# One branch over two rare paths, tiles normalised into PSUM, and constant products ahead of mixer two

## The chip, the cores and the metric

The kernel runs on one core of one Trainium2 chip. Its time is device microseconds from start to end of one execution; several executions were timed, and one more was taken with the hardware profiler. The engines are TensorE (PE, and PEld for its weight loads), VectorE (DVE), ScalarE (ACT), GpSimd (POOL) and SyncE (SP, which here issues most DMAs). A "q" behind a name (ACTq) is that engine's sequencer: branches, register loads, semaphore events.

## The reference

A trunk of two layers on 512 tokens of 1024 values, all in float32. Each layer is a mixer and a mixture of experts, each followed by a layer norm of the scaled input plus the result:

```python
for layer in range(2):
    mix = mixer[layer](x)                  # layer 0: convolutions; layer 1: gated blocks and chunked attention
    x = layer_norm(ALPHA * x + mix, mix_ln_g[layer], mix_ln_b[layer])
    ffn = hierarchical_moe(x, ...)         # 4 groups x 8 experts, one group, the best 2 experts of it
    x = layer_norm(ALPHA * x + ffn, ffn_ln_g[layer], ffn_ln_b[layer])

hb = silu(xb @ w_gate[e]) * (xb @ w_up[e]) # one expert: 1024 -> 512
y  = hb @ w_down[e]                        # 512 -> 1024; summed with the routing weights
layer_norm(x, g, b) = (x - mean) * rsqrt(var + 1e-5) * g + b
```

Which expert gets how many tokens depends on the data.

## The kernel before, in words

All 512 tokens stay in SBUF as four tiles of 128 tokens (`acc`, tiles t = 0 to 3). The 32 experts of a layer are taken as 16 pairs, g = 0 to 15, and every expert has 64 places for tokens. A pair is: gate products `pg` (`proj2`, L748, its products at L746), up products `pu`, the hidden values (`hidden`, L759), their transposes and eviction to `hT` by ScalarE (`hidden_T`, L764 to L769), and down products `py` (`down`, L772 to L780). In between TensorE spreads the previous pair's results back to the tokens (`combine` and `spread`, L788 to L799), and VectorE adds them to `acc`. The expert weights stream in from HBM on SP's queue, several pairs ahead.

An expert with more than 64 tokens needs extra work, and the routing counts how much, on the chip. Two pieces of code are there for it, and both are behind a branch on such a count. `overflow` (the branch at L1156, `skip`) handles a little more for one pair; the branch stands in every pair from g = 2 on, between the hidden transposes and the down products. `crowded` (from L1035, the branch at L1037) is a general loop over all pairs for what exceeds even that; it stands once per layer, before the gate products of g = 15. In the data timed here neither is needed in the last pair of a layer: the branches jump over the code. The counts lie in a row `nxi` in SBUF; each engine loads its count into a register, and the value `most`, the largest count for the general loop, is loaded at the end of g = 14 (L1164), along with a hint to TensorE's instruction fetch (`mark_branch_hint_location`). For the pairs the hint stands ahead of `pu` (L1135).

After the branch at L1037 `last()` follows: in layer 0 it issues the loads of two weight arrays of mixer two (`last0`, L1606) on SP's queue; in layer 1, constants of the last norm. `Last` (L801 to L830) finishes the sums of the last pair, with tiles 0 and 1 accumulated in PSUM by way of an identity product, and the statistics of the norm. `hat` (L281) writes the normalised values of a tile by ScalarE. Then come mixer two (L1328), whose `turn` (L1335) transposes the normalised tiles as input to its products, or, after layer 1, `output` (L1583): scale and shift by `gf` and `bf` on GpSimd and VectorE and the stores. GpSimd does tile 0 and three quarters of tile 1 (`PQ` is 256), VectorE the last quarter and tiles 2 and 3, on ScalarE's and SP's store queues.

`keep_warm` (L145) multiplies a constant with itself into a PSUM tile that nobody reads.

The order of each engine's instructions is the order in which the code is written. An instruction waits on semaphores for its inputs and for the release of the buffers it writes; behind a branch, a waiter waits for the event with which an engine closes it.

Of the kernel before, what the change touches and what calls it, by code (L numbers as in the profile page):

```python
# [10 lines left out]
I32 = mybir.dt.int32  # L11
# [17 lines left out]
NTHR = 6  # L29
WIDE = 3  # L30
CM = 1
PQ = 256
W0 = 10
W3 = 0
W4 = 0
# [8 lines left out]
def trunk(ctx: ExitStack, tc: tile.TileContext, a, out, layers=2, moe=True):  # L44
# [18 lines left out]
    def ptile(tag, shape=(128, 512)):  # L63
        return mtile(shape) if tag == "m" else ps.tile(list(shape), F32, name="p" + tag, tag=tag)

    def small(shape, name, dt=F32, **kw):
        return wk.tile([128] + list(shape), dt, name=name, **kw)
# [77 lines left out]
    def keep_warm(n, tag="m"):  # L145
        p = ptile(tag)
        for _ in range(n):
            PE.matmul(p, onesb[:, 0:1].to_broadcast([128, 128]), onesb[:, 0:1].to_broadcast([128, 512]), start=True, stop=True)
# [293 lines left out]
    class Router:  # L442
# [178 lines left out]
        def counts(self):  # L621
            c = self.rk[:, NT]
            big = wk.tile([128, NE, NE], F32, name="big", tag="xb")
            TT(big, self.at, bc(c[:, None, :], [NE, NE]), op=OP.mult)
            cs = small([NP, 2], "cs", tag="rcb")
            DVE.tensor_reduce(cs.rearrange("p g two -> p (g two)"), big, axis=AX.X, op=OP.add)
            over = small([2, NP, 2], "over", tag="scr")
            for i in range(2):
                TT(over[:, i], cs, lim[:, i], op=OP.is_gt)
            nxs = small([2 * NP + 1], "nxs")  # L630
            n, m = nxs[:, 0:NP], nxs[:, NP:2 * NP]
            mxc = small([NP], "mxc", tag="mxc")
            DVE.tensor_reduce(mxc, over[:, 1], axis=AX.X, op=OP.max)
            DVE.scalar_tensor_tensor(n, over[:, 0, :, 1], 2.0, over[:, 0, :, 0], op0=OP.mult, op1=OP.add)
            DVE.scalar_tensor_tensor(n, mxc, float(WIDE), n, op0=OP.mult, op1=OP.max)
            TS(n[:, HEAVY:HEAVY + 1], over[:, 0, HEAVY:HEAVY + 1, 1], float(WIDE), None, op0=OP.mult)
            mxe = small([NP], "mxe", tag="mxc")
            DVE.tensor_reduce(mxe, c.rearrange("p (g two) -> p g two", two=2), axis=AX.X, op=OP.max)
            nx = small([NP, NTHR], "nx", tag="scr")
            TT(nx, bc(mxe[:, :, None], [NP, NTHR]), bc(thr[:, None, :], [NP, NTHR]), op=OP.is_gt)  # L640
            DVE.tensor_reduce(m, nx, axis=AX.X, op=OP.add)
            for g in FIRST:
                DVE.scalar_tensor_tensor(m[:, g:g + 1], mxe[:, g:g + 1], float(CAP), m[:, g:g + 1], op0=OP.is_gt, op1=OP.add)
            DVE.tensor_reduce(nxs[:, 2 * NP:], m, axis=AX.X, op=OP.max)
            nxi = small([2 * NP + 1], "nxi", I32)
            DVE.tensor_copy(nxi, nxs)
            return nxi

# [99 lines left out]
    def proj2(tag, xt, wa, wb, own=EVEN[0]):  # L748
        p = ptile(tag)
        for k in range(KD):  # L750
            by_slots(p, xt[:, k], (wa[:, k], wb[:, k]), own, start=(k == 0), stop=(k == KD - 1))
        return p
# [6 lines left out]
    def hidden(sg, pu):  # L759
        h = wk.tile([128, 512], F32, name="h", tag="q1")  # L760
        DVE.tensor_mul(h, sg, pu)  # L761
        return h

    def hidden_T(h):  # L764
        p = mtile((128, 4, 128))
        for j in range(4):
            PE.transpose(p[:, j], h[:, j * 128:(j + 1) * 128], ident)  # L767
        hT = wk.tile([128, 4, 128], F32, name="hT", tag="q2")
        ACT.activation(hT, p, AF.Copy)  # L769
        return hT  # L770

# [11 lines left out]
    def onehot_S(tk, tag="q3"):  # L783
        S = wk.tile([128, T], F32R, name="S", tag=tag)
        TS(S, io, tk, None, op0=OP.is_equal)
        return S
# [6 lines left out]
    def combine(S, yh, yl, ts=range(NT)):  # L793
        for t in ts:
            for h in range(2):
                s = slice(h * 512, (h + 1) * 512)
                p = mtile()
                spread(p, S, yh, yl, t, h)
                DVE.tensor_add(acc[:, t, s], acc[:, t, s], p)  # L799
# [31 lines left out]
    def combine_last(last, mid=None):  # L831
        return last.ys, last.mrs + last.finish(2, mid)
# [135 lines left out]
    ET = mybir.EngineType  # L968

    def count(nxi, i, **kw):  # L970
        return nc.values_load(nxi[0:1, i:i + 1], min_val=0, max_val=NTHR + 1,
                              skip_runtime_bounds_check_because="a count of blocks", **kw)

    def when(nxi, i, above, engines=None):
        v = count(nxi, i, **({} if engines is None else {"engines": engines}))
        return v, tc.If(v > above)

    def experts(rt, ws, T1, pt, x1d, xt, xg, xg2, update, last, last2, lead, finish):
# [55 lines left out]

        def crowded():  # L1035
            slots = ws.order[6:8]
            with tc.If(most > 0, label=f"most{ws.l}", preferred_fallthrough_block=True):  # L1037
                for g in range(NP):
                    v, cond = when(nxi, NP + g, 0)
                    with cond:  # L1040
                        cur = small([2, NT], "cur")
                        R3, yh, yl = (wk.tile([128, D], F32R, name="room", tag=t) for t in ("l1", "xt1", "lng"))
                        R3 = R3.rearrange("p (j t m) -> p j t m", j=2, t=NT)
                        TS(cur, rt.r, 0.0 if g in FIRST else -float(CAP), None, op0=OP.add)
                        with tc.For_i(0, v, 1):
                            TS(cur, cur, -float(CAP), None, op0=OP.add)
                            rt.onehot(R3, range(NT), cur)
                            T3 = Table(rt, R3)
                            T3.one(2 * g)
                            gather(xg, x1d, T3.idx[:, 0:1])  # L1050
                            xo = gather_T(xg, rt.gb, wk.tile([128, KD, 128], F32, name="xo", tag="xb"))
                            u = [ws.fetch(0, j, slots[j], g) for j in range(2)]
                            h3 = gated(proj2("g", xo, *u))
                            u = [ws.fetch(0, 2 + j, slots[j], g) for j in range(2)]
                            h3 = hidden_T(hidden(h3, proj2("u", xo, *u)))
                            u = [ws.fetch(0, 4 + j, slots[j], g) for j in range(2)]
                            y3 = down(h3, *u, T3.wt[:, 0:1], (yh, yl))
                            combine(onehot_S(T3.tk[:, 0:1], "q2"), *y3)

        for g in range(NP):  # L1060
            W = lambda j: ws.u[6 * g + j]
            own, own2 = EVEN if COLS[g] < HEAVY else ODD
            if g == NP - 1:
                crowded()
                last()
            skip = f"skip{ws.l}_{g}"
            sg = gated(proj2("g", xt, W(0), W(1), own))
            if g == 0:
# [62 lines left out]
                h2 = wk.tile([128, 128], F32, name="h2", tag="r")  # L1131
                ACT.activation(h2, proj1("g", xo, W(0), b), AF.Silu)
            if g > 1:
                v = count(nxi, COLS[g])
                tc.mark_branch_hint_location(skip, v > 0, engines=[ET.PE])  # L1135
            pu = proj2("u", xt, W(2), W(3), own)
            h = hidden(sg, pu)
# [16 lines left out]
                down1(hT2, W(4), tw[:, 1:2], tw[:, 0:1])  # L1154
            if g > 1:
                with tc.If(v > 0, label=skip, preferred_fallthrough_block=True):  # L1156
                    overflow(v)
            ws.load(6 * g + 4 + 9)
            if g == NP - 1:
                last2()  # L1160
            if 0 < g < NP - 1:
                gather2(g + 1)
            if g == NP - 2:
                most = count(nxi, 2 * NP)  # L1164
                tc.mark_branch_hint_location(f"most{ws.l}", most > 0, engines=[ET.PE])
            if g == NP - 1:
                S = onehot_S(col(T1.tk, g))
            if g < NP - 1:
# [159 lines left out]
    def mixer1(prev, ws):  # L1328
# [29 lines left out]
                    ACT.activation(hi, x2[:, e], AF.Copy)  # L1358
                (DVE, POOL)[j % 2].tensor_tensor(lo, x2[:, e], hi, op=OP.subtract)

        ys, mrs = combine_last(prev, lambda: turn(0))
        TS(bq, par1[:, 4:8], 0.125, None, op0=OP.mult)
        gf, bf = (wk.tile([128, D], F32, name="gf", tag=t) for t in ("lng", "lnb"))
        rows = []
# [218 lines left out]
    def output(prev):  # L1583
        gf, bf = st["gf"], st["bf"]
        ys, mrs = combine_last(prev)

        def put(q, t, s):
            q.dma_start(out[t * 128:(t + 1) * 128, s], acc[:, t, s])

        def scale_shift(e, t, s):  # L1590
            x = acc[:, t, s]
            e.tensor_tensor(x, x, gf[:, s], op=OP.mult)  # L1592
            e.tensor_tensor(x, x, bf[:, s], op=OP.add)  # L1593
            put(nc.scalar, t, s)
        for t, s in ((0, slice(0, 512)), (0, slice(512, 1024)), (1, slice(0, 512)), (1, slice(512, 512 + PQ))):
            scale_shift(POOL, t, s)
        scale_shift(DVE, 1, slice(512 + PQ, 1024))
        for t in (2, 3):
            for h in range(2):
                s = slice(512 * h, 512 * h + 512)  # L1600
                x = acc[:, t, s]
                DVE.scalar_tensor_tensor(x, ys[t][h], mrs[t][0], gf[:, s], op0=OP.subtract, op1=OP.mult)  # L1602
                DVE.scalar_tensor_tensor(x, x, mrs[t][1], bf[:, s], op0=OP.mult, op1=OP.add)  # L1603
                put(nc.sync, t, s)

    def last0():  # L1606
# [103 lines left out]
```

## Time and profile before

| | us |
|---|---|
| three runs | 1438.19, 1443.88, 1445.37; median 1443.88 |
| the profiled execution | 1442.83, of which the profiled span 1440.9 |
| TensorE busy | 1333.4 (93% of the span) |
| VectorE, ScalarE, GpSimd busy | 684.5, 370.3, 294.7 |
| mean granted TensorE clock | 0.976 of full speed |
| read from HBM | 461.56 MB, 325 GB/s over the span |

A busy share is a mean over stages: in the expert stretches (about 220 to 690 us and 940 to 1420 us) TensorE and the weight stream both run almost without a break, in the mixers the other engines matter more. An "issue" as the cause of idle time means that the profile shows nothing that the engine waited for.

### The profile page before, as it was taken

The page shows a single profiled execution, that of the slowest core. Times are in us where ns is not written, and L with a number is a line of the kernel's source. Part 1 is how long each engine was busy: PE and PEld are TensorE (multiplying, and loading weights), DVE is VectorE, ACT ScalarE, POOL GpSimd, SP SyncE. Part 2 cuts the span into 40 slices and gives each one's busy share as a digit, 9 for nine tenths or more (in the row PEclk, how much of TensorE's full clock was granted, in tenths as well). Part 3 has the DMA queues.
Part 4 walks back from the last instruction along what each step waited for, and adds up shares of the span by engine and source line. Part 5 has one row for each costly group of instructions (what it writes and reads, how often), then busy time and mean ns, then how long its engine had stood idle before and what let it go on. Part 6 is the DMA issues. An engine that isn't in the chain of part 4 may idle for free. (4 is left out here: it accounts for less than half of the span.)

```text
span 1440.9 us, 19633 instructions
## 1 busy us (share of the span) xinstructions
PE 1333.4 (93%) x7322; PEld 705.9 (49%) x7322; DVE 684.5 (48%) x1412; ACT 370.3 (26%) x701; POOL 294.7 (20%) x262
## 2 busy tenths in 40 slices
PE   9989999998999998898899999999999999989984
PEld 6777764333353334333586767834333444333331
DVE  7997688323342223322628554794322343322326
ACT  5545541111111111111525555511111111111101
POOL 5784620000000000000653239200000000000002
PEclk9999999999999999999999999999999999999997
DMA  7505469999999999999500037689999999999971
GB/s 294 234 5 212 175 243 428 419 424 422 419 403 412 422 419 426 422 418 354 206 1 1 23 133 315 257 338 421 420 425 424 421 394 420 427 422 422 423 301 59
DMA packets 56837, 461.21 MB, mean 320 GB/s; under 512 B 8804, under 2 KB 9444, under 8 KB 33232
## 3 DMA queue, kind: packets, MB, share of 16 engines
q1 hardware_dynamic: 51184, 449.96, 75.8%
q0 software_dynamic: 4608, 7.79, 1.5%
q8 instruction: 102, 1.67, 0.5%
q10 hardware_dynamic: 864, 1.13, 0.2%
q14 instruction: 79, 0.65, 0.1%
HBM read 461.56 MB, written 6.29 MB: 325 GB/s over the span
## 5 line engine op out<-in xcount | busy, mean ns | idle before, releaser
L746 PE MATMUL py<-w,hT 128*64 128x512 f32 (+1 forms) x1280 | 243.2, 617 | 22.3 <-issue 11.6
L746 PE MATMUL pu<-w,xt 128*64 128x512 f32 (+1 forms) x1280 | 244.2, 607 | 19.8 <-DMA w<-in_w_up_dram 19.8
L746 PE MATMUL pg<-w,xt 128*64 128x512 f32 (+1 forms) x1280 | 233.4, 599 | 10.9 <-ACTq L1037 10.9
L761 DVE TENSOR_TENSOR h<-sg,pu 128x512 f32<-128x512 f32 x32 | 22.0, 688 | 355.9 <-issue 302.1
L691 POOL DMA_INDIRECT xg<-x1d,idx x30 | 29.7, 990 | 780.2 <-PE m L439 677.9
L746 PEld LDWEIGHTS pu<-w,xt 128*64 128x64 f32 (+1 forms) x1280 | 78.3, 129 | 176.3 <-issue 143.2
L799 DVE TENSOR_TENSOR acc<-acc,m 128x512 f32<-128x512 f32 x240 | 148.6, 680 | 19.3 <-PE m L791 17.3
L746 PEld LDWEIGHTS pg<-w,xt 128*64 128x64 f32 (+1 forms) x1280 | 76.2, 128 | 163.1 <-issue 140.8
L746 PEld LDWEIGHTS py<-w,hT 128*64 128x64 f32 (+1 forms) x1280 | 72.4, 128 | 154.5 <-issue 150.4
L780 DVE SCALAR_TENSOR_TENSOR y<-py,wt,y 128x512 fp32r<-128x512 f32 x64 | 48.0, 750 | 199.2 <-ACT y L779 199.2
L779 ACT ACTIVATE y<-py,wt 128x512 fp32r<-128x512 f32 x64 | 44.0, 687 | 302.9 <-PE py L746 302.9
L790 PE MATMUL m<-y,S 128*128 128x512 f32 x248 | 106.1, 428 | 0.0
L791 PE MATMUL m<-y,S 128*128 128x512 f32 x248 | 98.0, 395 | 0.0
L109 POOL TENSOR_TENSOR wl<-win,wh 128x512 fp32r<-128x512 f32 x64 | 84.2, 1331 | 65.6 <-ACT wh L108 65.4
L769 ACT ACTIVATE hT<-m 128x512 f32<-128x512 f32 x32 | 19.1, 597 | 292.4 <-PE m L767 270.5
L109 POOL TENSOR_TENSOR wl<-wo,wh 128x512 fp32r<-128x512 f32 x64 | 82.1, 1309 | 38.2 <-ACT wh L108 37.8
L756 ACT ACTIVATE sg<-pg 128x512 f32<-128x512 f32 x32 | 19.1, 597 | 217.3 <-PE pg L746 217.3
L790 PEld LDWEIGHTS m<-y,S 128*128 128x128 f32 x248 | 46.8, 189 | 39.3 <-issue 26.9
L128 PE MATMUL m<-xh,wl 128*128 128x512 f32 x144 | 57.6, 400 | 3.0 <-POOL wl L109 3.0
L127 PE MATMUL m<-xh,wh 128*128 128x512 f32 x144 | 57.4, 399 | 0.8 <-ACT wh L108 0.8
L129 PE MATMUL m<-xl,wh 128*128 128x512 f32 x144 | 56.8, 394 | 0.0
L791 PEld LDWEIGHTS m<-y,S 128*128 128x128 f32 x248 | 46.9, 189 | 7.9 <-DVE y L780 1.0
(446 smaller groups left out, 1881.2 us busy)
## 6 DMA issues: line engine op xcount, KB each, us to landing
w<-in_w_gate_dram SPq DMA_DIRECT2D x64, 2048.0 KB, 24.9
w<-in_w_up_dram SPq DMA_DIRECT2D x50, 2048.0 KB, 18.2
w<-in_w_down_dram SPq DMA_DIRECT2D x50, 2048.0 KB, 21.0
w<-in_w_up_dram SPq DMA_DIRECT2D x40, 512.0 KB, 25.0
w<-in_w_down_dram SPq DMA_DIRECT2D x40, 512.0 KB, 22.8
win<-in_w_in_dram SPq DMA_DIRECT2D x18, 512.0 KB, 7.8
wo<-in_w_out_dram SPq DMA_DIRECT2D x4, 2048.0 KB, 12.3
w<-in_w_up_dram SPq DMA_DIRECT2D x8, 1024.0 KB, 15.8
```

The source lines that it names most:

```text
L109: POOL.tensor_tensor(l, src, h, op=OP.subtract)
L127: PE.matmul(p, wh[:, j], xh[:, k], start=(k == 0), stop=False)
L128: PE.matmul(p, wl[:, j], xh[:, k], start=False, stop=False)
L129: PE.matmul(p, wh[:, j], xl[:, k], start=False, stop=(k == KD - 1))
L691: POOL.indirect_dma_start(out=dst, out_offset=None, in_=x1d, in_offset=bass.IndirectOffsetOnAxis(ap=idx_col, axis=0), bounds_check=T - 1, ...
L746: PE.matmul(p[w * c:w * c + w], x[:, w * c:w * c + w], ww[own[w * c // SUB]], **kw)
L761: DVE.tensor_mul(h, sg, pu)
L779: ACT.activation(yh[:, s], p, AF.Copy, scale=wt)
L780: DVE.scalar_tensor_tensor(yl[:, s], p, wt, yh[:, s], op0=OP.mult, op1=OP.subtract)
L790: PE.matmul(p, S[:, t * 128:(t + 1) * 128], yh[:, s], start=start, stop=False)
L791: PE.matmul(p, S[:, t * 128:(t + 1) * 128], yl[:, s], start=False, stop=True)
L799: DVE.tensor_add(acc[:, t, s], acc[:, t, s], p)
```

## The change

Three parts.

1. The count row gets one more value, `most` plus the count of the last pair (`nxs[2 * NP + 1]`, one more VectorE addition in each layer's routing). The branch before `pg` of g = 15 and the count and hint for it at g = 14 go. At g = 15 the overflow branch tests the new value and holds both pieces: the pair's overflow under a second test, and the general loop under its own. `last()` stands behind that branch. Two tags in code that isn't executed here change, so that its buffers do not collide with live ones.
2. In mixer two ten `keep_warm` products stand ahead of the first `turn`.
3. In `output` ScalarE normalises the four halves of tiles 2 and 3 into four PSUM banks with one activation each (scale 1/std, bias -mean/std), VectorE multiplies by `gf` in PSUM and adds `bf` into `acc`, and GpSimd does both halves of tiles 0 and 1.

```diff
-            nxs = small([2 * NP + 1], "nxs")
+            nxs = small([2 * NP + 2], "nxs")
...
+            TT(nxs[:, 2 * NP + 1:], nxs[:, 2 * NP:2 * NP + 1], n[:, COLS[-1]:COLS[-1] + 1], op=OP.add)
...
         def crowded():
             slots = ws.order[6:8]
-            with tc.If(most > 0, label=f"most{ws.l}", preferred_fallthrough_block=True):
+            with when(nxi, 2 * NP, 0)[1]:
...
-            if g == NP - 1:
-                crowded()
-                last()
             skip = f"skip{ws.l}_{g}"
...
-                v = count(nxi, COLS[g])
+                v = count(nxi, COLS[g] if g < NP - 1 else 2 * NP + 1)
                 tc.mark_branch_hint_location(skip, v > 0, engines=[ET.PE])
...
                 with tc.If(v > 0, label=skip, preferred_fallthrough_block=True):
-                    overflow(v)
+                    if g < NP - 1:
+                        overflow(v)
+                    else:
+                        v1, cond = when(nxi, COLS[g], 0)
+                        with cond:
+                            overflow(v1)
+                        crowded()
+                if g == NP - 1:
+                    last()
...
-            if g == NP - 2:
-                most = count(nxi, 2 * NP)
-                tc.mark_branch_hint_location(f"most{ws.l}", most > 0, engines=[ET.PE])
...
-        ys, mrs = combine_last(prev, lambda: turn(0))
+        def first_turn():
+            keep_warm(10)
+            turn(0)
+        ys, mrs = combine_last(prev, first_turn)
...
-        for t, s in ((0, slice(0, 512)), (0, slice(512, 1024)), (1, slice(0, 512)), (1, slice(512, 512 + PQ))):
-            scale_shift(POOL, t, s)
-        scale_shift(DVE, 1, slice(512 + PQ, 1024))
+        norms = {}
+        for t in (2, 3):
+            for h in range(2):
+                p = norms[t, h] = ptile("gu"[h] if t == 2 else f"y{h}")
+                ACT.activation(p, ys[t][h], AF.Identity, bias=mrs[t][2], scale=mrs[t][1])
+        for t in (0, 1):
+            for h in range(2):
+                scale_shift(POOL, t, slice(512 * h, 512 * h + 512))
         for t in (2, 3):
             for h in range(2):
                 s = slice(512 * h, 512 * h + 512)
-                x = acc[:, t, s]
-                DVE.scalar_tensor_tensor(x, ys[t][h], mrs[t][0], gf[:, s], op0=OP.subtract, op1=OP.mult)
-                DVE.scalar_tensor_tensor(x, x, mrs[t][1], bf[:, s], op0=OP.mult, op1=OP.add)
+                p = norms[t, h]
+                TT(p, p, gf[:, s], op=OP.mult)
+                TT(acc[:, t, s], p, bf[:, s], op=OP.add)
                 put(nc.sync, t, s)
```

The first place is TensorE at the end of pair 14 and in pair 15 of layer 1, before (`py` with `hT` are down products, the first `py` of pair 14, the last of pair 15; a landing is the row at which a skipped branch comes out):

```order
L971 TENSOR_LOAD nxi
L1165 REGISTER_ALU
L1706 BRANCH_PREFETCH_HINT
L746 MATMUL py_25295<-w,hT 64x512 x8
...
L1037 COMPARE_AND_BRANCH
...
L1037 UNCONDITIONAL_BRANCH
L746 MATMUL pg<-w,xt 64x512 x16
...
L1156 COMPARE_AND_BRANCH
...
L1156 UNCONDITIONAL_BRANCH
L746 MATMUL py_28935<-w,hT 64x512 x8
```

and the same stretch now (the overflow branch has line 1153 there):

```order
L746 MATMUL py_25333<-w,hT 64x512 x8
L746 MATMUL pg<-w,xt 64x512 x16
...
L1132 REGISTER_ALU
L1716 BRANCH_PREFETCH_HINT
L746 MATMUL pu<-w,xt 64x512 x16
...
L767 MATMUL m<-ident,h 128x128 x4
L1153 COMPARE_AND_BRANCH
...
L1037 UNCONDITIONAL_BRANCH
L1153 UNCONDITIONAL_BRANCH
L746 MATMUL py_28958<-w,hT 64x512 x8
```

The branch at L1037 and its landing have moved from ahead of `pg` into the overflow branch behind the transposes, and the two register operations and the hint at pair 14 are gone. From branch to landing it was 513 rows of this list for the general loop and 40 for the overflow; now it is 558 for both together.

The second place is TensorE at the start of mixer two, now (`acc` is the normalised tile, `onesb` the constant; before, the last spread of layer 0 is followed by the transposes at once):

```order
L791 MATMUL py_14352<-y,S 128x512
L147 LDWEIGHTS onesb
L147 MATMUL m<-onesb 128x512
...
L1343 MATMUL m<-ident,acc 128x128 x16
L1382 MATMUL m<-wh,xh 128x512
```

The ten pairs of weight load and product are new; nothing else has changed its place there.

The third is VectorE at the end of the kernel, before (`mvr` and `mv` hold the statistics of tiles 2 and 3, `gf` and `bf` the last norm's scale and shift):

```order
L275 SCALAR_TENSOR_TENSOR mvr<-mv_29012,mvr 128x2
L1592 TENSOR_TENSOR acc<-acc,gf 128x256
L1593 TENSOR_TENSOR acc<-acc,bf 128x256
L1602 SCALAR_TENSOR_TENSOR acc<-acc,mv_29012,gf 128x512
L1603 SCALAR_TENSOR_TENSOR acc<-acc,mvr,bf 128x512
```

and now:

```order
L274 SCALAR_TENSOR_TENSOR mvr<-mv_29035,mvr 128x2
L1612 TENSOR_TENSOR pg<-pg,gf 128x512
L1613 TENSOR_TENSOR acc<-pg,bf 128x512
L1612 TENSOR_TENSOR pu<-pu,gf 128x512
L1613 TENSOR_TENSOR acc<-pu,bf 128x512
```

with the last of these on ScalarE:

```order
L259 ACTIVATE mvr<-mv_29035,quarter 128x2
L1604 ACTIVATE pg<-acc,mvr 128x512
L1604 ACTIVATE pu<-acc,mvr 128x512
L1604 ACTIVATE py_29050<-acc,mvr 128x512
L1604 ACTIVATE py_29052<-acc,mvr 128x512
L1593 DMA out_dram<-acc 128x512 x4
```

VectorE's two operations on a quarter of tile 1 have gone to GpSimd, its eight on tiles 2 and 3 (two of four pairs are shown) read a PSUM bank, and ScalarE's four store instructions now stand behind four activations.

## Rows read from the trace of the kernel before

**Rows 1.** The longest waits: engine, line, releaser, total us, times, longest.

```profile
PE pu L746 <- DMA w<-in_w_up_dram: 19.8, 9, 4.4
...
PE py L746 <- issue: 11.6, 5, 3.2
```

**Rows 2.** TensorE's timeline, layer 0: start, us, operation, idle before.

```profile
642.37 2.73 PE L746 MATMUL py<-w,hT 128*64 128x512 f32 x10 [2.72 <-issue]
...
655.17 8.46 PE L746 MATMUL pg<-w,xt 128*64 128x512 f32 x32 [5.45 <-ACTq L1037]
...
665.62 7.09 PE L746 MATMUL pu<-w,xt 128*64 128x512 f32 x32
...
675.94 1.51 PE L746 MATMUL py<-w,hT 128*64 128x512 f32 x6 [0.74 <-ACTq L1156]
```

**Rows 3.** The same, layer 1.

```profile
1371.12 3.65 PE L746 MATMUL py<-w,hT 128*64 128x512 f32 x16 [0.86 <-PEq L1156]
...
1384.82 8.86 PE L746 MATMUL pg<-w,xt 128*64 128x512 f32 x32 [5.44 <-ACTq L1037]
...
1405.98 1.51 PE L746 MATMUL py<-w,hT 128*64 128x512 f32 x6 [0.74 <-ACTq L1156]
```

**Rows 4.** The branch line L1037: ns least, median, most, first and last start.

```profile
L1037 ACTq EVENT_SEMAPHORE  x4: 17/17/17, 655.1 to 1384.8; - x4
...
L1037 PEldq COMPARE_BRANCH  x2: 2867/4458/6049, 646.1 to 1375.7; - x2
L1037 ACTq COMPARE_BRANCH  x2: 45/45/45, 649.8 to 1379.5; - x2
...
  DVE S L785: 10.1, 2
```

**Rows 5.** The overflow branch's line L1156, likewise.

```profile
L1156 ACTq COMPARE_BRANCH  x28: 45/45/45, 271.3 to 1405.4; - x28
L1156 ACTq EVENT_SEMAPHORE  x28: 17/17/17, 271.9 to 1406.0; - x28
```

**Rows 6.** Two stretches: us, busy of PE, PEld, DVE, ACT, POOL, granted clock, DMA, GB/s.

```profile
655.17:663.63 8.46, 8.46 (x33) 2.62 (x33) 0.48 (x1) 0.00 (x0) 0.00 (x0) 0.83 0.87 313
693.98:698.63 4.65, 3.64 (x17) 3.45 (x18) 4.51 (x11) 3.89 (x7) 0.35 (x1) 0.67 0.98 372
```

**Rows 7.** DMA issues from 1371.9 to 1372.5: KB, us to landing.

```profile
w<-in_w_up_dram SPq DMA_DIRECT2D x1, 1024.0 KB, 15.7
```

**Rows 8.** TensorE's timeline, layer 1, pair 9.

```profile
1222.64 1.45 PE L746 MATMUL py<-w,hT 128*64 128x512 f32 x5 [2.10 <-issue]
```

**Rows 9.** TensorE's timeline at the start of mixer two.

```profile
693.98 0.33 PE L1341 MATMUL m<-ident,acc 128*128 128x128 f32 x1 [3.25 <-ACT acc L284]
695.32 3.31 PE L1341 MATMUL m<-ident,acc 128*128 128x128 f32 x15 [1.01 <-ACT acc L284]
...
715.00 0.51 PE L1378 MATMUL m<-wl,xh 128*128 128x512 f32 x1 [2.49 <-POOL wl L109]
```

**Rows 10.** The constant products' line L148.

```profile
L148 PE MATMUL m<-onesb x20: 377/494/632, 0.9 to 931.2; 128*128 128x512 bf16 x20
```

**Rows 11.** All engines' timeline of the end.

```profile
1423.16 1.26 POOL L1592 TENSOR_TENSOR acc<-acc,gf 128x512 f32<-128x512 f32 x1 [78.99 <-ACT acc L284]
...
1427.43 0.91 DVE L275 SCALAR_TENSOR_TENSOR mvr<-mv,mvr 128x2 f32<-128x2 f32 x1
...
1430.00 1.75 DVE L1602 SCALAR_TENSOR_TENSOR acc<-acc,mv,gf 128x512 f32<-128x512 f32 x1
...
1436.94 0.75 DVE L1603 SCALAR_TENSOR_TENSOR acc<-acc,mvr,bf 128x512 f32<-128x512 f32 x1
```

**Rows 12.** VectorE's additions of spread results, by line (us, mean ns).

```profile
L799 DVE TENSOR_TENSOR acc<-acc,m 128x512 f32<-128x512 f32 x240 | 148.6, 680 | 19.3 <-PE m L791 17.3
```

**Rows 13.** VectorE's subtraction on SBUF alone.

```profile
L120 DVE TENSOR_TENSOR xl<-xT,xh x8: 680/692/1820, 5.4 to 14.2; 128x512 fp32r<-128x512 f32 x8
```

**Rows 14.** ScalarE's scaling from SBUF into PSUM.

```profile
L312 ACT ACTIVATE py<-apad,par x2: 782/782/783, 22.9 to 58.6; 128x512 f32<-128x512 f32 x2
```

More of the change, by code (lines that the diff above doesn't have):

```diff
@@ L31 @@
 CM = 1
-PQ = 256
 W0 = 10
@@ L643, in counts @@
                 DVE.scalar_tensor_tensor(m[:, g:g + 1], mxe[:, g:g + 1], float(CAP), m[:, g:g + 1], op0=OP.is_gt, op1=OP.add)
-            DVE.tensor_reduce(nxs[:, 2 * NP:], m, axis=AX.X, op=OP.max)
-            nxi = small([2 * NP + 1], "nxi", I32)
+            DVE.tensor_reduce(nxs[:, 2 * NP:2 * NP + 1], m, axis=AX.X, op=OP.max)
+            TT(nxs[:, 2 * NP + 1:], nxs[:, 2 * NP:2 * NP + 1], n[:, COLS[-1]:COLS[-1] + 1], op=OP.add)
+            nxi = small([2 * NP + 2], "nxi", I32)
             DVE.tensor_copy(nxi, nxs)
@@ L762, in hidden, with hidden_T @@
         return h
-    def hidden_T(h):
+    def hidden_T(h, tag="q2"):
         p = mtile((128, 4, 128))
@@ L767, in hidden_T @@
             PE.transpose(p[:, j], h[:, j * 128:(j + 1) * 128], ident)
-        hT = wk.tile([128, 4, 128], F32, name="hT", tag="q2")
+        hT = wk.tile([128, 4, 128], F32, name="hT", tag=tag)
         ACT.activation(hT, p, AF.Copy)
@@ L970, in count @@
     def count(nxi, i, **kw):
-        return nc.values_load(nxi[0:1, i:i + 1], min_val=0, max_val=NTHR + 1,
+        return nc.values_load(nxi[0:1, i:i + 1], min_val=0, max_val=NTHR + 1 + WIDE,
                               skip_runtime_bounds_check_because="a count of blocks", **kw)
@@ L1054, in crowded @@
                             u = [ws.fetch(0, 2 + j, slots[j], g) for j in range(2)]
-                            h3 = hidden_T(hidden(h3, proj2("u", xo, *u)))
+                            h3 = hidden_T(hidden(h3, proj2("u", xo, *u)), "q3")
                             u = [ws.fetch(0, 4 + j, slots[j], g) for j in range(2)]
                             y3 = down(h3, *u, T3.wt[:, 0:1], (yh, yl))
-                            combine(onehot_S(T3.tk[:, 0:1], "q2"), *y3)
+                            combine(onehot_S(T3.tk[:, 0:1], "r"), *y3)
         for g in range(NP):
```

## The prediction, made before the changed kernel ran

> **What bounds the kernel now.** I read the waits first: in the expert stretch TensorE waits longest for up weights (19.8 us over 9 times) and, named "issue", ahead of down products (11.6 over 5) [rows 1]. Then its own timeline at the last pair of each layer, where it stands 5.45 and 5.44 us before `pg` and 0.74 before the last `py`, each time released by ScalarE's queue [rows 2, 3]. The views of the two branch lines say why. At L1037 ScalarE's branch is at 649.8 and its closing event at 655.1, in layer 1 at 1379.5 and 1384.8: 5.3 us for a branch that is skipped [rows 4]. At L1156 it takes 0.6 (271.3 to 271.9, 1405.4 to 1406.0) [rows 5]. Both jump over code that isn't run; the general loop is long, an overflow block short. Behind the far jump the granted clock is low for a while: `pg` takes 8.46 and 8.86 us, the first at a mean clock of 0.83, where the 32 `pu` products take 7.09 [rows 2, 3, 6]. Last the end of the kernel: VectorE works alone from the last statistics to the last store, 1437.69 [rows 11]. TensorE is busy nearly everywhere else, so the change is worth what it does at these places, at pair 14 and at the start of mixer two.
>
> **The branch, layer 0.** Removed: the stand of 5.45 before `pg`, and the 1.37 (8.46 - 7.09) that the low clock costs behind it [rows 2]; the down products of pair 14 now run straight into `pg`. Added: at the overflow branch every engine now jumps over the overflow block and the general loop together. That is a far jump as before, over more code on each engine, and `py` waits for ScalarE's event behind it. ScalarE branches when it has issued the eviction of `hT`, and `py` starts with its event; with 5.3 in place of 0.6 [rows 4, 5] the stand of 0.74 becomes 0.74 + 4.7 = 5.44. VectorE branches about then too, and its skipped far jump cost the `S` behind it 5.1 each [rows 4], so it is no later. TensorE's own jump took 2.9 and 6.0 [rows 4]; its hint now stands ahead of `pu`, whose 7.09 [rows 2] cover it. A stand as long as before will cost the clock again, now in `py`, whose half takes 3.65 in full [rows 3]: bounds 0 and 3.65 (all of it at half speed); I take the 1.4 that the like stand costs before `pg`. So -5.45 - 0.74 + 5.44 = **-0.75**, the clock even; bounds -2.1 and +1.5.
>
> SP passes the far branch later too, and `last()` stands behind it: the `val` weights of mixer two, and all that is queued on SP behind them, leave some 6 us later. At the start of mixer two TensorE is released by ScalarE's normalised halves, not by a transfer [rows 9]; I take 0. If that cover is gone, the 6 us show in front of the first split.
>
> **The branch, layer 1.** The same -0.75. Besides, pair 14 loses the count of `most` and its hint, which stood ahead of its down products: TensorE waits 0.86 there [rows 3], so **-0.86**. In layer 0 the same two go, but there a gap of 2.72 follows within the down products [rows 2], which I read as a fetch behind the skipped branch that ends at its own time, however early the products before it are: 0. Weights: the last up piece, issued at 1372.1, lands 15.7 later, at 1387.8 [rows 7]. Without the first stand `pg` runs from 1379.4 (1384.82 - 5.44) to 1386.5, the eight spreads to 1388.5 (2.0, as between `pg` and `pu` [rows 2]), and `pu` starts just behind its weights. They would stop a much larger gain, not this one. Layer 1 together **-1.6**.
>
> Its bounds are -3.4 (the clock's 1.77 not paid again) and +3.3 (a whole `py` half at half speed, +1.9, and 3 from moved code). Of the gaps named "issue", 3.2 is the longest and 2.10 the only one in layer 1 [rows 1, 8]. With the general loop moved behind, layer 1's products stand some twenty instructions further on, and such a gap can go or grow by 0 to 3.
> [...]
>
> **keep_warm(10).** Ten products on constants stand ahead of mixer two's first transposes. Their PSUM bank is one that the closing normalisation still reads, so the first waits for ScalarE's first normalised half, as the first transpose does now: TensorE stands 3.25, makes one at 693.98, stands 1.01 and makes 15 in 3.31, to 698.63, at a mean clock of 0.67 [rows 6, 9]. The gap of 3.25 isn't filled; the ten only come first. Such products (L148) take 494 ns in the median, and neighbours overlap [rows 10]. I bound one by 0.22 (32 `pu` products in 7.09 [rows 2]) and 0.49. At 0.22 they end at 696.2, and 16 transposes at 0.15 (3.31 / 15 x 0.67) end at 698.6, as today. At 0.49: 698.9, then 2.4 to 3.5, 702.4 at worst. VectorE needs only the first four, and feeds ScalarE's splits, GpSimd's `wl` and with it the products at 715.00, where TensorE waits 2.49 for `wl` [rows 9]; a delay goes on to there. I take **+0.5**, near the fast end since the products themselves keep the engine busy; bounds -0.7 and +2.5.
>
> **Output.** Before: the last statistics are there at 1428.3; VectorE does a quarter of tile 1, then eight operations on tiles 2 and 3, the first 1.75 long beside GpSimd, the last 0.75 without it, to 1437.69; the span ends 3.2 later [rows 11]. After: GpSimd does all of tiles 0 and 1. ScalarE normalises tiles 2 and 3 into PSUM, from 1428.4, at 0.78 each at most [rows 14]; the first half is there at 1429.2. Then eight VectorE operations with one operand in PSUM: 0.68 each (L799) [rows 12], where one on SBUF alone lies between 0.68 and 1.82 (L120) [rows 13]. GpSimd holds up the second kind; L799 runs beside no GpSimd arithmetic, so I add 0 to 0.1 for one that waits for the one before it. Pairs of 1.35 give 1429.2 + 4 x 1.35 = 1434.6, 3.1 earlier. GpSimd's eight at 1.26 to 1.35 from 1423.16 [rows 11] end by 1434.0; its stores queue on ScalarE behind the four activations and aren't last. So **-3.1**; bounds -3.6 and -1.5 (GpSimd at 1.5 each ends at 1435.2, and stores of two queues crowd). One more small VectorE operation in each routing, and a few stores on another queue, count as nothing; uncovered, 0.2 us each.
>
> **Sum.** -0.75 - 1.6 + 0.5 - 3.1 = -4.95 on the profiled run's 1442.83 (span 1440.9 and 1.9 around it): 1437.9. The median of the runs, 1443.88, lies 1.05 above that run; on its footing **1439.0**, -0.34%. No change is what lies within 0.5%, 7.2 us either way. The forecast's own range, by half of each bound, is 1434 to 1444.
>
> **Rivals.** A, *the far jump costs nothing any more*: what follows it is fetched while `pu` runs, `py` keeps its 0.74, and the stands before `pg` go with their slow clock: -5.45 - 1.37 - 5.44 - 1.77 = -14.0, with the rest -14.0 - 0.86 + 0.5 - 3.1 = -17.5, 1426.4. For it: TensorE's hint comes one `pu` earlier. Against: `py` waits for ScalarE and VectorE, which have no hint, and TensorE's hint did not help at L1037 [rows 4].
> B, *slower*: layer 1's moved products meet the gaps that layer 0 has. The five of 11.6 less the 2.1 that is there already [rows 1, 8] would add 9.5 and give -4.95 + 9.5 = +4.5, 1448.4. It decides once new gaps in layer 1 pass 5 us. For: all its down products move. Against: TensorE waits for up weights there [rows 1], and a gap ahead of such a wait is free.
> C, *constant products and output at their bad ends*: -0.75 - 1.6 + 2.5 - 1.5 = -1.35, 1442.5. For: the clock is low at that start [rows 6].
>
> **Chances.** Forecast 0.55, A 0.18, B 0.12, C 0.15. Faster by over 0.5%: A and 0.3 of the forecast, whose edge lies 2 us below its time, less than the runs differ among themselves (1438 to 1445): 0.35. Slower: the far half of B and the runs' spread, 0.08. The same: 0.57. The range 1427 to 1447 leaves out half of A and over half of B.
>
> **What would show it.** Right: no stand before the last `pg`; one near 5.4 before the last `py` in both layers, released by ScalarE's or VectorE's queue; no wait for TensorE's sequencer at pair 14 of layer 1; VectorE's last operation ending 6.3 us after the last statistics (1428.3 to 1434.6), not 9.4. Wrong: a `py` stand under 2 us (A); new "issue" gaps in layer 1 (B); mixer two's first product over 2 us later against its first normalised half, or GpSimd ending last (C).

## The result, and the profile after

The changed kernel took 1429.97 us (median of 5 runs, 1426.89 to 1433.18) beside 1443.88 before (5 runs): ratio 0.9909, 95% interval 0.9887 to 0.9932. The same kernel was timed twice more, with 0.9956 (0.9935 to 0.9977) and 0.9908 (0.9882 to 0.9934). Over all of it, 18 runs of the changed kernel average 1431.9 and 44 of before 1443.2: -11.2 us, ratio 0.9922, give or take 0.0013. The forecast was 1439.0, -0.34%: of the right sign, but less than half of what came. The result lies inside the stated range (1427 to 1447) and outside the forecast's own range (1434 to 1444).

Where it came from can be read from the starts of the same products in both traces. The table gives how much longer (+) or shorter (-) a stretch is than in the trace of before, in us, for three profiles of the changed kernel. There is one trace of before, so what was particular to that execution is in every column. "The product at 720" is the one that starts at 720.4 in it.

| stretch of TensorE's products | before | after | second profile | third | forecast |
|---|---|---|---|---|---|
| layer 0, second down half of pair 14 to the last spread | 44.27 | -4.46 | -3.12 | -2.99 | -0.75 |
| from there to the product at 720 (mixer two's start) | 30.06 | +0.62 | +0.48 | +0.46 | +0.5 |
| layer 1, `pu` of pair 14 to the last spread | 63.30 | -4.52 | -4.76 | -3.78 | -1.6 |
| last spread to the end (output) | 20.51 | -2.86 | -2.85 | -2.88 | -3.1 |
| sum | | -11.2 | -10.3 | -9.2 | -4.95 |

The sums stand near the -11.2 of the many runs. The first pair of traces differs by only 9.5 us in span (1440.9 and 1431.4): of the stretches that the change leaves alone, two cost 1.6 each more in it and two others 1.6 less together, and in the other profiles these come out otherwise. Two rows of the forecast hold, two don't, and both of these are the branch.

TensorE at the last pairs, after, layer 0 and then layer 1 (start, us, operation, idle before and its releaser):

```profile
650.23 7.04 PE L746 MATMUL pg<-w,xt 128*64 128x512 f32 x32
...
672.15 3.65 PE L746 MATMUL py<-w,hT 128*64 128x512 f32 x16 [3.30 <-ACTq L1153]
```

```profile
1354.96 7.08 PE L746 MATMUL pu<-w,xt 128*64 128x512 f32 x30 [0.63 <-DMA w<-in_w_up_dram]
...
1366.58 3.65 PE L746 MATMUL py<-w,hT 128*64 128x512 f32 x16
...
1374.68 7.55 PE L746 MATMUL pg<-w,xt 128*64 128x512 f32 x32
...
1397.68 5.33 PE L746 MATMUL py<-w,hT 128*64 128x512 f32 x16 [3.88 <-DVEq L1153]
```

Against [rows 2, 3]: the stand before `pg` is gone, the wait at pair 14 too, and the stand has moved to the last `py`, as forecast. But it is 3.30 and 3.88 long (2.96 and 3.10, 3.93 and 3.86 in the other two profiles), not 5.44. In layer 1 `py` then takes 5.33 at a mean granted clock of 0.68; in layer 0 it takes 3.65 at a clock of 1.00 here, but 5.35 in the other two profiles.

The branch line of the changed kernel, by narrow windows: layer 0 (SP's branch first, then the other engines'), and layer 1.

```profile
L1153 SPq EVENT_SEMAPHORE  x7: 17/17/17, 659.9 to 660.4; - x7
...
L1153 DVEq EVENT_SEMAPHORE  x2: 21/21/21, 671.9 to 672.0; - x2
L1153 ACTq EVENT_SEMAPHORE  x2: 17/17/17, 671.9 to 672.0; - x2
L1153 SPq COMPARE_BRANCH  x1: 45/45/45, 654.5 to 654.5; - x1
L1153 PEldq COMPARE_BRANCH  x1: 347/347/347, 667.8 to 667.8; - x1
L1153 DVEq COMPARE_BRANCH  x1: 56/56/56, 668.5 to 668.5; - x1
L1153 ACTq COMPARE_BRANCH  x1: 45/45/45, 668.9 to 668.9; - x1
```

```profile
L1153 ACTq EVENT_SEMAPHORE  x2: 17/17/17, 1396.8 to 1396.9; - x2
L1153 DVEq EVENT_SEMAPHORE  x2: 21/21/21, 1397.4 to 1397.5; - x2
...
L1153 DVEq COMPARE_BRANCH  x1: 56/56/56, 1393.4 to 1393.4; - x1
L1153 ACTq COMPARE_BRANCH  x1: 45/45/45, 1393.8 to 1393.8; - x1
```

ScalarE's far jump takes 3.0 in both layers, over more code than the 5.3 of [rows 4]; VectorE's 3.4 and 4.0; SP's, at 654.5, still 5.4. What differs is the memory traffic during the jump. The windows of these three, with the columns of [rows 6] (the last three are the clock, the DMA engines' share, GB/s):

```profile
668.90:671.90 3.00, 0.00 (x0) 0.00 (x0) 0.64 (x2) 0.58 (x1) 0.00 (x0) 1.00 0.71 180
1393.80:1396.80 3.00, 0.00 (x0) 0.00 (x0) 0.70 (x2) 0.60 (x1) 0.00 (x0) 1.00 0.13 42
654.50:659.90 5.40, 5.40 (x26) 2.49 (x24) 1.94 (x4) 0.60 (x1) 0.00 (x0) 1.00 1.01 373
```

Before, the two jumps at L1037 ran beside 365 and 395 GB/s of weights. At the new place the layer's weights are over, or nearly.

Other packets move during the jump too: the DMA view has queues of kind "instruction" (packets, MB, share of 16 engines). Before, layer 0, they move nothing from 649.8 to 652.3, the first 2.5 us of ScalarE's jump, and in the rest of it, from 652.3 to 655.1:

```profile
q8 instruction: 1, 0.02, 2.4%
q14 instruction: 2, 0.02, 1.8%
```

In the changed kernel the same three packets come in the first 1.3 us, from 668.9 to 670.2, and none after that:

```profile
q8 instruction: 1, 0.02, 6.1%
q14 instruction: 2, 0.02, 3.4%
```

The view doesn't say to which engine each of them belongs.

The output, VectorE's first and last operations after:

```profile
1420.80 0.91 DVE L274 SCALAR_TENSOR_TENSOR mvr<-mv,mvr 128x2 f32<-128x2 f32 x1
1422.62 0.70 DVE L1612 TENSOR_TENSOR pg<-pg,gf 128x512 f32<-128x512 f32 x1 [0.91 <-ACT pg L1604]
...
1427.35 0.69 DVE L1613 TENSOR_TENSOR acc<-py,bf 128x512 f32<-128x512 f32 x1
```

From the last statistics (1421.71) to the last result it is 6.33 us, where [rows 11] have 9.4. The eight take 0.69 to 0.70 each, the first six of them beside GpSimd, which works until 1426.8.

### The profile page after: what moved, and what is told of

It is laid out like the page before. It is cut to its first block, busy times and chain, and to the rows that moved or that the text cites. A ratio compares the mean times of both kernels' runs of the same rounds, so it can differ in the third digit from the quotient of the medians.

```text
span 1431.4 us, 19616 instructions
## 1 busy us (share of the span) xinstructions
PE 1333.5 (93%) x7332; PEld 706.2 (49%) x7332; DVE 679.2 (47%) x1412; ACT 373.9 (26%) x705; POOL 294.7 (21%) x262
## 5 line engine op out<-in xcount | busy, mean ns | idle before, releaser
L746 PE MATMUL py<-w,hT 128*64 128x512 f32 (+1 forms) x1280 | 245.6, 622 | 25.4 <-issue 10.3
L746 PE MATMUL pg<-w,xt 128*64 128x512 f32 (+1 forms) x1280 | 230.1, 594 | 0.5 <-DMA w<-in_w_gate_dram 0.5
L790 PEld LDWEIGHTS m<-y,S 128*128 128x128 f32 x248 | 46.7, 188 | 39.5 <-issue 26.9
L107 ACT ACTIVATE wh<-win 128x512 fp32r<-128x512 f32 x64 | 39.1, 625 | 51.0 <-PE pg L128 13.6
```

The costliest lines, as they stand in the source:

```text
L107: ACT.activation(h, src, AF.Copy)
L746: PE.matmul(p[w * c:w * c + w], x[:, w * c:w * c + w], ww[own[w * c // SUB]], **kw)
L790: PE.matmul(p, S[:, t * 128:(t + 1) * 128], yh[:, s], start=start, stop=False)
```

## The experiments

Kernels that were timed together share the runs of before; each ratio is against these.

**The changed kernel again**, for more profiles (no edit).

> The changed kernel once more, for a second profile. In the first pair of profiles the starts of TensorE's products moved by -4.5 us over the last pair of layer 0, -3.0 over pairs 14 and 15 of layer 1 and -2.9 in the output, but also by about +1.6 each in two stretches that the change leaves alone; medians differ by 13.9. Theory: those two are a matter of where the granted clock happened to fall, so here ScalarE's far jump again takes 3.0 us in both layers and the stands before the last py are 3 to 4, but the untouched stretches add up to something else, and the whole is 11 to 16 below before. Rival: the stretches after the change are slowed by it (code that moved); then the same +1.6 stand in the same places.

> The changed kernel a third time. Its two ratios so far are 0.9909 and 0.9956, and the parts read from two of its profiles add up to -10.3 and -11.2 us (0.993 to 0.992). Theory: the parts are what the change gives and the two medians scatter around them; so 0.991 to 0.995 again, ScalarE's far jump 2.9 to 3.2 and the output -2.9 as before. If the profiles' sum is not the whole, 0.990 or less.

Ratios 0.9956 and 0.9908. The first is about 6 us, less than the 11 to 16 expected. The parts are in the table; the stretches that had cost +1.6 each came out at -1.1 and +2.9 (up to pair 14 of layer 0) and 0.0 and 0.0 (within mixer two). They don't belong to the change. ScalarE's jump took 2.9 to 3.2 throughout. The third profile's parts add to -9.2, a little less than expected, since the low clock falls on both last `py` halves (1.7 and 2.85 over their 3.65).

**The branch alone** (constant products and output as before).

```diff
-        def first_turn():
-            keep_warm(10)
-            turn(0)
-        ys, mrs = combine_last(prev, first_turn)
+        ys, mrs = combine_last(prev, lambda: turn(0))
```

(and `output` as in the kernel before)

> Only the branch part of the change; mixer two and output as before. By the sum of the first traces -4.5 (layer 0) and -3.0 (layer 1), -7 to -9 in all, ratio 0.994 to 0.995. If constant products and output carry more than their -2.3, it is less, 0.996 to 0.998. By rival A as forecast (jump hidden) it would be -15, 0.990.

0.9953 (0.9935 to 0.9972), -6.8 us. Its two branch stretches give -2.7 and -5.4, the output +0.1, the start of mixer two +0.1. So in its profile the branch carries the larger part of the change, -8.0 in all as expected, and not rival A's -15; 5.2 us are lost in mixer two besides, of which more below.

**More traffic during the jump**: four loads of 2 MB per layer, into two free buffers, that nobody reads.

```diff
+            if g == NP - 1:
+                spare = [unit(ws.order[6 + j], [128, 8, 512], F32, "w") for j in range(2)]
+                for k in range(4):
+                    nc.sync.dma_start(spare[k % 2], a["w_gate"][ws.l * NE + k])
             if g > 1:
                 with tc.If(v > 0, label=skip, preferred_fallthrough_block=True):
```

> The changed kernel with four extra 2 MB loads per layer into two free buffers, queued on SP just ahead of the last pair's branch; nobody reads them. Theory: the far jump is a fetch of instructions that shares memory traffic with the weight stream. At L1037 before (365 to 395 GB/s on the way) it took ScalarE 5.3 us, at the new place (180 and 42 GB/s) 3.0, and SP, which makes the same jump earlier, under the full stream, still 5.4. So with the extra loads ScalarE's jump goes back to about 5.3 in both layers and the stand before the last py from 3.3 to 3.9 to 5.4 to 6. [...]

ScalarE's and VectorE's branch in layer 0 and then layer 1, and the windows of ScalarE's jumps:

```profile
L1157 ACTq EVENT_SEMAPHORE  x2: 17/17/17, 673.8 to 673.9; - x2
L1157 DVEq EVENT_SEMAPHORE  x2: 21/21/21, 674.6 to 674.7; - x2
...
L1157 DVEq COMPARE_BRANCH  x1: 56/56/56, 668.9 to 668.9; - x1
L1157 ACTq COMPARE_BRANCH  x1: 45/45/45, 669.4 to 669.4; - x1
```

```profile
L1157 ACTq EVENT_SEMAPHORE  x2: 17/17/17, 1407.0 to 1407.0; - x2
...
L1157 ACTq COMPARE_BRANCH  x1: 45/45/45, 1401.2 to 1401.2; - x1
```

```profile
669.40:673.80 4.40, 0.00 (x0) 0.00 (x0) 0.62 (x2) 0.56 (x1) 0.00 (x0) 0.71 0.98 369
1401.20:1407.00 5.80, 0.00 (x0) 0.00 (x0) 0.70 (x2) 0.60 (x1) 0.00 (x0) 0.84 0.99 401
```

Same code, same place (only SP has four instructions more): ScalarE's jump went from 3.0 to 4.4 and 5.7, VectorE's from 3.4 and 4.0 to 5.6 and 6.2, and `py` stands 5.62 and 6.05. In layer 0 ScalarE's 4.4 is short of the expected 5.3. The instruction packets of queue 14, 0.8 and 0.9 us behind ScalarE's branch in the changed kernel, come only from 672.0 on:

```profile
q14 instruction: 2, 0.02, 2.4%
```

The single run took 1443.86, as long as before the change; 3.5 us of that are lost at the start of mixer two, whose own weights are issued 12 us later behind these loads. Had the place in the code decided alone, ScalarE's jump would have stayed at 3.0, so that cause falls: the same jump took 3.0 beside 180 and 42 GB/s, and 4.4 and 5.7 beside 369 and 401. That it is a fetch of instructions is the author's reading of the packets; what it shares with the other transfers isn't told apart. There is one execution, but it shows the effect in both layers, and in the nine other profiles with a far jump at this place ScalarE's took 2.7 to 3.2. This is the experiment that settles the main step.

**Hints on ScalarE and VectorE too.**

```diff
-                tc.mark_branch_hint_location(skip, v > 0, engines=[ET.PE])
+                tc.mark_branch_hint_location(skip, v > 0, engines=[ET.PE] if g < NP - 1 else [ET.PE, ET.Activation, ET.DVE])
```

> The changed kernel with the prefetch hint of the last pair's branch on ScalarE and VectorE too, not on TensorE alone. If the far jump is a fetch of instructions, ScalarE's 3.0 us fall to under 1 and py stands 0.7 to 1.2 in place of 3.3 to 3.9: -5 to -7 on the changed kernel (the second with the clock that layer 1 then does not lose). If the hint does nothing on these engines (as TensorE's own jump at L1037 still took 2.9 to 6.0 with one), no change.

```profile
L1153 ACTq EVENT_SEMAPHORE  x2: 17/17/17, 670.5 to 670.5; - x2
...
L1153 ACTq COMPARE_BRANCH  x1: 64/64/64, 667.4 to 667.4; - x1
```

No change: ScalarE 3.1, VectorE 3.2 in layer 0 and 3.0 and 4.0 in layer 1, though the hint stands ahead of `pu`. Ratio 0.9944 (0.9928 to 0.9960), like the changed kernel beside it. The hope for a better version fell.

**No hint for TensorE.**

```diff
-                tc.mark_branch_hint_location(skip, v > 0, engines=[ET.PE])
+                if g < NP - 1:
+                    tc.mark_branch_hint_location(skip, v > 0, engines=[ET.PE])
```

> The changed kernel without the prefetch hint for TensorE at the last pair. With it TensorE's own branch takes 0.35 us and 1.1 to its event in both layers. Theory: the hint is what keeps TensorE out of it, without it TensorE's jump takes about 3 as ScalarE's and starts 1 us earlier, so py stands the same 3.3 to 3.9. Rival: TensorE's far jump is longer without a hint than ScalarE's (over 4), then py stands that much longer.

```profile
L1154 ACTq EVENT_SEMAPHORE  x2: 17/17/17, 670.2 to 670.3; - x2
L1154 PEldq COMPARE_BRANCH  x1: 3731/3731/3731, 666.2 to 666.2; - x1
```

TensorE's own branch takes 3.7 in place of 0.35, and still ends before ScalarE's event; `py` stands 3.27 (layer 1: 3.93) as with the hint; the single run took 1433.81. On TensorE the hint does work here, but it hides a jump that ScalarE's and VectorE's would cover anyway (events at 670.2 and 670.0, TensorE's at 670.0).

**No general loop behind the last pair's branch** (left out: the code for experts over their last places, which these data don't run).

```diff
-                        crowded()
+                        pass
```

> The changed kernel with the general loop's code left out of the last pair's branch (it is not executed with these data, so only the jump gets short). Theory, the length of what is jumped over decides: ScalarE's jump takes 0.6 as at the other pairs, py stands 0.7, -5 to -7 on the changed kernel. Rival, the stand is made by the two nested tests or by last() behind the branch: py still stands 3 us or more.

The last `py` in layer 0, in layer 1, and TensorE's waits for down products:

```profile
667.82 3.65 PE L746 MATMUL py<-w,hT 128*64 128x512 f32 x16 [0.69 <-ACTq L1153]
...
1400.47 5.35 PE L746 MATMUL py<-w,hT 128*64 128x512 f32 x16 [2.89 <-PEq L1153]
```

```profile
PE py L746 <- issue: 18.3, 7, 3.4
```

In layer 0 the length of the jump decides, as expected: the stand is 0.69, 2.6 less. In layer 1 `py` still stands, now for TensorE's own branch, which took 3.46 though it is a short one and has the hint. And the gaps named "issue" grew from 11.6 over 5 [rows 1] to 18.3 over 7, 8.7 of it in layer 1, where before there was one of 2.1 [rows 8]: in a kernel whose code has moved, as rival B had it; what they wait for no view shows. From the end of mixer two to `pu` of pair 14 layer 1 took 3.3 longer, not 6.6, since TensorE waited less for the layer's up weights (6.1 against 13.4). Ratio 0.9934 (0.9910 to 0.9958), not to be told from the changed kernel. Half of the expectation missed: the far jump costs 2.6 in layer 0, but what taking it away gained doesn't show in the whole, where these 3.3 and another 4.0 in mixer two (see below) stand against it.

**Constant products in another bank, or none.**

```diff
-            keep_warm(10)
+            keep_warm(10, "g")
```

> The changed kernel with the ten constant products of mixer two written to the bank of the gate products, which is free by then, in place of one that the closing normalisation still reads. Theory: the wait for that bank is why they cost 0.4 us instead of helping; now they run in the gap of 3.25 us ahead of the first normalised half, that half's transposes start at the same time as before the change, and mixer two's first product comes 0.5 to 1.5 us earlier against the last spread than in the changed kernel (8.1 us from last spread to first product goes to 7). On the whole time at most -0.1%, not to be told from nothing. Rival: the products don't keep the clock up; no difference from a kernel without them.

> The kernel with the constant products in the gate bank again, beside the changed kernel on the same chip. From the last spread of layer 0 to the product at 720 of before it should again take 29.6 us, 0.9 less than the changed kernel; on the whole 0.991 to 0.995 too, at most 0.1% below the changed kernel. Its first profile had VectorE's product of the routing weights at 2.91 us in place of 0.66, beside GpSimd, and 5.1 us lost there; theory: that is a chance of phase and need not come again. Rival: it belongs to this code, then it stands there again.

> The changed kernel without the constant products. From the last spread of layer 0 to the product at 720 of before: 30.1 us as in the branch alone and before, against 30.5 with the products (30.7 where the low clock falls there). So -0.4 us on the changed kernel, nothing that the whole time shows. If they did help, it gets longer here.

The start of mixer two with the bank of the closing norm (second profile of the changed kernel), with the gate bank (first and second profile), and without the products:

```profile
686.47 2.35 PE L147 MATMUL m<-onesb 128*128 128x512 bf16 x9 [3.25 <-ACT acc L283]
688.66 1.91 PE L1343 MATMUL m<-ident,acc 128*128 128x128 f32 x16
```

```profile
681.65 2.36 PE L147 MATMUL pg<-onesb 128*128 128x512 bf16 x10
...
686.40 1.86 PE L1343 MATMUL m<-ident,acc 128*128 128x128 f32 x15 [1.01 <-ACT acc L283]
```

```profile
692.37 2.93 PE L1343 MATMUL m<-ident,acc 128*128 128x128 f32 x15 [1.01 <-ACT acc L283]
```

```profile
692.27 3.08 PE L1343 MATMUL m<-ident,acc 128*128 128x128 f32 x15 [1.01 <-ACT acc L283]
```

In the changed kernel the products stand behind the 3.25 gap; in the gate bank they fill it. In the first profile the 15 transposes then take 1.86 at a granted clock of 1.00, against 3.08 at 0.57 without the products; in the second they take 2.93 at 0.60, although the products filled the gap as before. So the products did not keep the clock up each time. From the last spread to mixer two's first product it is 7.4 and 7.6 in the gate bank (7 was expected), 7.7 without products, 7.9 before the change and 8.1 in the changed kernel (9.7 in its first profile, where the low clock falls there: 0.63 over the constant products, 0.80 over the transposes). To the product at 720 it is 29.65 in the gate bank, 29.8 without products (30.1 before and in the branch alone), 30.5 to 30.7 in the changed kernel; the second profile of the gate bank had 28.1 there, but with the low clock on the `py` before and 1.6 later in mixer two, so it is no clean reading. So as placed by the change the products cost 0.4 to 0.9; in the free bank they cost nothing that can be seen, and what they gain, 0.1 to 0.5 in one profile, is hardly more than the 0.3 by which kernels without them differ. On the whole the two timings, 0.9909 (0.9888 to 0.9931) and 0.9914 (0.9882 to 0.9945), and 0.9933 (0.9909 to 0.9957) without products, can't be told from the changed kernel.

All of these (branch alone, no loop, gate bank twice, none) lose 4 to 5 us in mixer two, at one place where before and the changed kernel, in all its three profiles, lose nothing: VectorE's product of the routing weights, in the second profile with the gate bank, and the wait behind it on TensorE.

```profile
874.33 3.54 DVE L471 TENSOR_TENSOR rwg<-rw,gb 128x288 f32<-128x288 f32 x1 [1.81 <-DMA gb<-in_lncol_dram]
...
880.54 0.53 PE L476 MATMUL m<-sums,onesf 128*128 128x72 f32 x2 [3.97 <-DVE sums L474]
```

In these five profiles the product takes 2.9 to 4.2; in the changed kernel it took 0.55 to 1.05, and 0.66 before. Here it runs beside six GpSimd operations in a row (871.3 to 879.0), with both inputs in SBUF; TensorE then waits 4.0, and the 128x512 products behind the wait take 0.63 each, where such a product (L1203) takes 0.40 in the median of the changed kernel. But it runs beside the same row of six in every profile, also where it is short, as in the changed kernel, where the row lasts from 873.0 to 881.0:

```profile
876.07 1.05 DVE L471 TENSOR_TENSOR rwg<-rw,gb 128x288 f32<-128x288 f32 x1 [1.80 <-DMA gb<-in_lncol_dram]
```

So GpSimd's row alone is not the cause. The theory of chance is weakened, since it came back in the same kernel; why it comes in just these five profiles is open.

## Why the prediction came out as it did

**Which wait goes and where it comes again: right.** The stand before `pg` went whole (from the last `py` of pair 14 to `pg` it is 5.6 less in both layers), most of the clock's loss behind it too (-1.4 in layer 0, -1.3 to -1.7 in layer 1; the mean clock of `pg` was 0.83 and 0.80 before and is 1.00 in both layers of the first profile), and a stand came before the last `py`, released by ScalarE's and VectorE's events, as the sum had it. That VectorE is no later than ScalarE was wrong: in layer 1 its event comes 0.4 to 0.7 behind ScalarE's and releases `py` in all three profiles. Rival A, that the jump would be hidden, is refuted: TensorE's part of it is hidden by the hint (its branch takes 0.35 with it, 3.7 without), the others' is not (3.0 on ScalarE, 3.4 and 4.0 on VectorE).

**Its size: wrong, and this is the step that failed.** The prediction put "5.3 in place of 0.6" and so 5.44 before `py`. It took the far jump's price from L1037 as a property of the jump. Measured are 3.30 and 3.88, because ScalarE's jump took 3.0 and VectorE's, which releases `py` in layer 1, 4.0. The trace of before had the other half of the answer: during the last `pu` of layer 1 the DMA's share is down to 0.44 and 165 GB/s,

```profile
1395.66:1402.75 7.09, 7.09 (x34) 2.28 (x33) 1.19 (x2) 0.00 (x0) 0.00 (x0) 1.00 0.44 165
```

while during the two jumps at L1037 it was 0.96 and 1.01. In layer 0 the `val` weights filled that stretch before (0.97 and 401 GB/s from 664 to 673), and the change itself puts them behind the last branch. They leave later, but not because SP passes the far branch later, as the prediction had it: SP is through at 660.4, and then waits for the event with which TensorE closes that branch,

```profile
SPq L1619 <- PEq L1153: 8.4, 1, 8.4
```

so the first of them is issued at 668.97, inside ScalarE's jump, where before it was issued at 662.74. The extra loads brought a stand of 5.6 and 6.05 back. The far jump explains 2.1 and 1.6 of the difference between forecast and first profile.

**The clock even: near in four of six cases.** The low clock comes back in `py` (0.68 over the 5.33 of the first profile): it costs 1.7, 1.45 and 2.85 in layer 1, and in layer 0 1.7 in two of three profiles of the changed kernel and 0 in one, where it came at the start of mixer two instead. Against the 1.3 to 1.7 that went before `pg`, the two that are not near are the 0 and the 2.85.

**Pair 14 of layer 1: right, but more hung on it.** The 0.86 went. Another 1.55 went with it in every profile with the change: before, `pu` of pair 14 stood 2.74 for its weights and then took 8.78 for 30 products, at a mean clock of 0.81; after, it stands 0.63 and takes 7.08 at 1.00. But the low clock falls in the pair before it now (0.81 there, where it was 1.00). Pairs 13 and 14 before, then pair 13 in the changed kernel:

```profile
1326.65 7.06 PE L746 MATMUL pu<-w,xt 128*32 128x512 f32 x60 [1.81 <-DMA w<-in_w_up_dram]
...
1357.09 8.78 PE L746 MATMUL pu<-w,xt 128*64 128x512 f32 x30 [2.74 <-DMA w<-in_w_up_dram]
```

```profile
1324.94 8.76 PE L746 MATMUL pu<-w,xt 128*32 128x512 f32 x60 [3.51 <-DMA w<-in_w_up_dram]
```

Before, the 30 `pu` products of pair 12 also took 8.78; in all three profiles of the changed kernel they take 7.08, pair 13 waits longer and runs slow, and TensorE comes to pair 14 when its weights are nearly there. These pairs wait for weights in any case, and the table's row of layer 1 starts behind that wait, at pair 14: it counts the loss that is gone there and not the one that came at pair 13. Whether the change takes away one slow pair of two, or the one trace of before was slow in an odd place, is open.

**Constant products: right** (+0.5, measured +0.5 to +0.6 against before), with its reason, the wait for the bank. **Output: right** (-3.1, measured -2.9), with its reason: the operations with one operand in PSUM take 0.69 to 0.70 beside GpSimd, pairs of 1.34 where 1.35 was taken.

**Rival B** did not show in the changed kernel: "issue" gaps before its down products are 10.1 to 10.3, not 11.6, and none of them is in layer 1, where the 2.10 of [rows 8] is gone. Longer gaps of this kind with moved code are there in the kernel without the loop: 18.3 over 7.

One correction to the description ahead of the prediction: in layer 1 `last()` does nothing; the last norm's constants are loaded by `last2()`, which stood behind the overflow branch before the change too.

The sum of the errors: 2.1 + 1.6 for the far jump in the first profile (2.5 + 1.5 and 2.3 + 1.6 in the others) and 1.55 at pair 14. The clock at the last pair adds 1.4 in layer 0 of the first profile; elsewhere it takes away 0.1 to 0.4, and 1.15 in layer 1 of the third. Together they make up, to some tenths, the 4 to 6 us between the forecast's sum and those of the profiles.

**The range: luck.** The result is inside 1427 to 1447 because that range made room for rival A, which is refuted; the time came between A and the forecast by a jump that is shorter, not hidden. The likeliest outcome was put as no change beyond 0.5%, at 0.57; what came, -0.65 to -0.91% over all runs, was put at 0.35.

## What to carry to other kernels

A price read in one stage holds for that stage's traffic: ScalarE's far jump took 5.3 us beside 365 and 395 GB/s and 3.0 beside 180 and 42. So before moving a branch over long code, look at what the DMA does at the new place. A rare path cost its jump here even when skipped (0.6 us for the short one, 2.7 to 5.7 for the far one on ScalarE), and the engine whose event was waited for decided, not the one that carries the hint. And filler products whose bank was still being read came behind the gap of 3.25 us that they were to fill; in a free bank they filled it, but no gain was clear of the differences between profiles.

## What the runs showed of the hardware

- A skipped far branch took ScalarE 3.0 us beside 180 and 42 GB/s of transfers (2.7 to 3.2 at that place over nine profiles), 5.3 beside 365 and 395 at L1037, and 4.4 and 5.7 beside 369 and 401 with the extra loads; a short one 0.6. At the last pair VectorE's took about as long to 1.2 us longer.
- During such a jump two packets of the instruction queue 14 move: in the changed kernel they start within 1.4 us of ScalarE's branch, before the change and with the extra loads only 2.5 us or more behind it.
- With the prefetch hint TensorE's far branch took 0.35 us at the last pair, without it 3.7; at L1037, with a hint, it took 2.9 and 6.0 [rows 4]. On ScalarE and VectorE it changed nothing (3.1 and 3.2 in layer 0 with it, 3.0 and 3.4 without).
- VectorE's product of the routing weights, on two SBUF operands, took 0.66 us before and 3.54 in the second profile of the gate bank, each time beside the same row of six GpSimd operations; its eight operations with one operand in PSUM took 0.69 to 0.70 at the end of the changed kernel, six of them beside GpSimd.
